# Moving the hgrn readout, the convolution and the low parts of some weights in a one-core encoder layer

## Chip, cores and metric

The kernel runs on one core of a Trainium2 chip. The metric is the device time of one execution in microseconds (us); the time before is the median of three runs.

## What is computed

One layer of a streaming encoder on 256 tokens of width 2048, all in float32. Cut to what matters here:

```
xn = rms_norm(x, g_mix)
cb, cc, ch, hq, hf, hi, hg, aq, ak, av, gate_a, gate_b, gate_c = split(xn @ w_in)
y_conv = cb * causal_depthwise_conv(cc * ch, conv_w)          # width 1024
y_hg   = hgrn2(hq, hf, hi, hg, ...)                           # width 1024
y_att  = chunk_band_attention(aq, ak, av, rel_bias)           # width 1024
merged = (sigmoid(gate_a) * (y_conv @ w_branch[0])
        + sigmoid(gate_b) * (y_hg   @ w_branch[1])
        + sigmoid(gate_c) * (y_att  @ w_branch[2]))           # width 2048
h = x + merged @ w_o
h = h + square(relu(rms_norm(h, g_ff) @ w_ff1)) @ w_ff2
h = h + sigmoid(rms_norm(h, g_ple) @ w_ple_gate) * (p @ w_ple_in)
out = rms_norm(h, g_final)
```

## The kernel before

**Arithmetic.** A float32 product is made of three matmuls in a narrower format: each operand is split into a high part (a rounded copy, made on ACT) and a low part (the operand less its high part, one subtraction on DVE), and the product is high x high + high x low + low x high (`mm_b` and `mm3`, lines 269 to 294). Activations are split once and kept (XN holds 16 blocks of 128 rows, each 256 tokens of high and 256 of low parts). Weights are split as they come.

**The weight stream.** The host packs all weights in the order of use (`units`, line 44). A unit is 128 x 1024 numbers, two units are one load of 1024 KB, issued by SP into one of three `raw` buffers (lines 165, 179). `Stream.unit` (line 162) splits a unit: ACT writes `hi` (line 192), DVE writes `lo` (line 193, by the helper of line 132). There are five buffers of each. `prod_a` (line 239) makes a 128-row block of columns from two units, `prod_t` and `prod_h` make rows of tokens. Each engine works through its instructions in a fixed order, which the framework draws up when the kernel is built from the order of the program and its own estimates of the durations; neighbouring pieces of work are therefore interleaved.

**Half a gate.** `prod_h` (line 346) multiplies XN by one half (1024 columns) of a gate's weights, in eight pairs of 128-row blocks, into PSUM banks: four `c`, and four `y` for the pairs in SEVEN = (1, 2, 4, 6). The other pairs are plain: two units of 12 matmuls each. A pair in SEVEN goes by `seven` (line 309): the 2 x 2 product of blocks (two row blocks by two column blocks) in seven block products instead of eight, with 21 matmuls. For that DVE forms differences of the weights (`tw`, lines 322, 327, 328) and four sets of low parts, and uses sums of activation blocks XS (`forms`, line 336), made once. It takes four of the hi and lo buffers. At the end of a half eight DVE operations combine c and y into `o` (lines 366 to 372).

**Stages.** First, in two groups of four heads, the projections for hgrn and attention with both computations beside them as side work (`side`, `step`). The attention outputs end each group (lines 687 to 694), and p1 and the PSUM pools are released. Then the convolution: eight blocks (lines 705 to 719), each with three products by `prod_a`, each result multiplied by rstd (`scaled`, line 462), which stands for the normalization's scale that XN does not yet hold. Then side work `rescale` (line 722) multiplies XN by rstd, splits it again in place and makes XS. Then the merge (lines 747 to 773): for the branches hg, at, cv in this order and two halves each, the gate's half by `prod_h(XN)`, its sigmoid on ACT, the branch's readout (`prod_h(branch, 4)`, eight plain units) and the product into `m`. In the first half the readout comes ahead of the gate, and ACT copies it into `m` (line 754). The output projection, the feed-forward part and the rest follow, and the change doesn't touch them.

`wide` and `narrow` take 2 KB tiles of the pool `ev` in turn (eight buffers).

Of the kernel before, what the change touches and what calls it, by code (L numbers as in the profile page):

```python
# [33 lines left out]
HALF = D // 2  # L34
GATES = ((1, "hg"), (2, "at"), (0, "cv"))

SEVEN = (1, 2, 4, 6)


C_CB, C_CC, C_CH, C_HQ, C_HF, C_HI, C_HG, C_AQ, C_AK, C_AV = [1024 * i for i in range(10)]  # L40
# [3 lines left out]
def units():  # L44

    def tile_a(name, row, col, n):
        return [("a", name, row + 1024 * j, col) for j in range(n)]

    def pair_a(name, row, c0, c1):
        return [("a", name, row, c0), ("a", name, row, c1),
                ("a", name, row + 1024, c0), ("a", name, row + 1024, c1)]

    def tile_b(name, col, row=0, n=8):
        return [("b", name, row + 256 * j, col) for j in range(n)]  # L60

    def half_b(name, col, row=0, n=8, seven=()):

        for g in range(n):
            r = row + 256 * g
            if g in seven:
                yield "c", name, (r, col), (r, col + 512)
                yield "c", name, (r + P, col + 512), (r + P, col)
            else:
                yield "b", name, r, col  # L70
                yield "b", name, r, col + 512

    out = []
    for g in range(2):
        out += tile_b("w_in", C_HI + 512 * g)
        for h in range(4 * g, 4 * g + 4):
            for c in (C_HQ, C_HF, C_HG):
                out += tile_a("w_in", 0, c + P * h, 2)
        for h in range(4 * g, 4 * g + 4):
            for c in (C_AQ, C_AK):  # L80
                out += tile_a("w_in", 0, c + P * h, 2)
        out += tile_b("w_in", C_AV + 512 * g)
    for i in range(8):
        for c in (C_CC, C_CH, C_CB):
            out += tile_a("w_in", 0, c + P * i, 2)
    for j, _ in GATES:
        for h in range(2):
            two = [half_b("w_in", (C_GA, C_GB, C_GC)[j] + HALF * h, seven=SEVEN),
                   half_b("w_branch", HALF * h, j * CW, 4)]
            for part in two[::-1] if j == GATES[0][0] and h == 0 else two:  # L90
                out += part
    for c in range(NC):
        out += tile_b("w_o", 512 * c)
    for f in range(NFG):
        out += pair_a("w_ff1", 0, f * 2048, f * 2048 + P)
        for i in range(2, FT):
            out += tile_a("w_ff1", 0, f * 2048 + P * i, 2)
        for c in range(NC):
            out += tile_b("w_ff2", 512 * c, f * 2048)
            if f == PLE_AT:  # L100
                out += tile_b("w_ple_in", 512 * c, 0, 1)
    for c in range(NC):
        out += tile_b("w_ple_gate", 512 * c)
    return out
# [3 lines left out]
def encoder_kernel(ctx: ExitStack, tc: tile.TileContext, xT, xtok, pT, wst, gains, gfin, convw, lblog,  # L108
# [4 lines left out]
    cst = ctx.enter_context(tc.tile_pool(name="cst", bufs=1))  # L113
    wp = ctx.enter_context(tc.tile_pool(name="wp", bufs=5))
    big = ctx.enter_context(tc.tile_pool(name="big", bufs=1))
    ev = ctx.enter_context(tc.tile_pool(name="ev", bufs=8))
    PS = bass.MemoryType.PSUM
    acc = tc.alloc_tile_pool(name="acc", bufs=4, space=PS, reuse_waits="tile")
    bgp = tc.alloc_tile_pool(name="bgp", bufs=2, space=PS, reuse_waits="tile")
# [29 lines left out]
    class Stream:  # L149
# [9 lines left out]
            self.n += 2  # L159
            return raw.rearrange("p a b -> p (a b)")  # L160

        def unit(self, hi=None, lo=None):
            r, half = divmod(self.n, 2)
            if half == 0:
                self.raw = wp.tile([P, 2, 1024], F32, name="raw", bufs=3)
                if r == 0:
                    for k in range(4):
                        a, b = divmod(k, 2)
                        w = slice(512 * b, 512 * b + 512)
                        nc.sync.dma_start(self.raw[:, a, w], wst[0, :, 512 * k:512 * k + 512])  # L170
                        if k == 0:
                            nc.sync.dma_start(gn, gains)
                        load_x(k, 1)
                elif r < 4:
                    for j in range(2):
                        load_x(4 * r + 2 * j, 2)
                        nc.sync.dma_start(self.raw[:, j, :], wst[r, :, 1024 * j:1024 * j + 1024])
                else:
                    nc.sync.dma_start(self.raw, wst[r].rearrange("p (a b) -> p a b", a=2))
            self.n += 1  # L180
            raw = self.raw[:, half, :]
            if hi is None:
                hi = wp.tile([P, 1024], F32R, name="hi")
            if lo is None:
                lo = wp.tile([P, 1024], F32R, name="lo")
            m = 2 if r < 4 else 1
            for j in range(m):
                w = slice(1024 // m * j, 1024 // m * (j + 1))
                if r < 4:
                    k = 4 * r + 2 * half + j  # L190
                    split(XN[:, k, :], xr[:, k, :], g_mix[:, k:k + 1])
                S.activation(hi[:, w], raw[:, w], AF.Copy)  # L192
                tt(lo[:, w], raw[:, w], hi[:, w].bitcast(F32), ALU.subtract)
            return hi, lo
# [148 lines left out]
        S.activation(xs[:, 0:4, :], f, AF.Copy)  # L343
        tt(xs[:, 4:8, :], f, xs[:, 0:4, :].bitcast(F32), ALU.subtract)

    def prod_h(x, n=8, xs=None):


        c = [acc.tile([P, 512], F32, name="ps") for _ in range(4)]
        y = None  # L350
        for g in range(n):
            if xs is not None and g in SEVEN:
                if y is None:
                    y = [acc.tile([P, 512], F32, name="ps") for _ in range(4)]
                seven(c, y, x, 2 * g, xs[SEVEN.index(g)], g == SEVEN[0], g == SEVEN[-1])
                step()
            else:
                for h in range(2):
                    unit = nxt()
                    for t in range(2):  # L360
                        mm_b(c[2 * t + h], unit, x, 2 * g, t, first=g == 0, last=g == n - 1)
                    step()
        if xs is None:
            return c
        o = [wide("o") for _ in range(4)]
        S.activation(o[0], y[0], AF.Copy)
        tt(o[1], y[2], o[0], ALU.add)
        tt(o[2], y[3], o[1], ALU.add)
        tt(o[1], y[1], o[1], ALU.add)
        tt(o[3], y[1], o[2], ALU.add)  # L370
        for i in range(4):
            tt(o[i], c[i], o[i], ALU.add)
        return o
# [327 lines left out]

    late = tc.alloc_tile_pool(name="late", bufs=1, reuse_waits="tile")
    p2 = tc.alloc_tile_pool(name="p2", bufs=1, reuse_waits="tile")
    ycv = late.tile([P, 8, 512], F32R, name="ycv", tag="c16")
    for i in range(8):
        u = p2.tile([P, 2 * T], F32, name="u")
        y = narrow("z")
        cc = wide()[:, 0:T]
        G.memset(u[:, 0:2], 0.0)
        scaled(cc)  # L710
        scaled(u[:, 2:T + 2])
        tt(u[:, 2:T + 2], u[:, 2:T + 2], cc, ALU.mult)
        V.tensor_scalar(y, u[:, 2:T + 2], cw[:, 2, i:i + 1], None, op0=ALU.mult)
        V.scalar_tensor_tensor(y, u[:, 1:T + 1], cw[:, 1, i:i + 1], y, op0=ALU.mult, op1=ALU.add)
        V.scalar_tensor_tensor(y, u[:, 0:T], cw[:, 0, i:i + 1], y, op0=ALU.mult, op1=ALU.add)
        cb = wide()[:, 0:T]
        scaled(cb)
        tt(y, y, cb, ALU.mult)
        split(ycv[:, i, :], y)
    XS = [p2.tile([P, 8, P], F32R, name=f"XS{i}") for i in range(len(SEVEN))]  # L720

    def rescale():

        for g in range(NK // 2):
# [8 lines left out]
                forms(XS[SEVEN.index(g)], a)  # L733
            yield

    side.append(rescale())

    M = [None] * 2

# [3 lines left out]
        S.activation(hi, pt, AF.Copy)  # L743
        tt(m[:, k:k + 2, T:2 * T], pt, hi.bitcast(F32), ALU.subtract)

    m = p2.tile([P, 2, D], F32, name="m")
    for i, (_, y) in enumerate(GATES):
        for h in range(2):
            first = i == h == 0
            branch = {"hg": yhg, "at": yat, "cv": ycv}[y]  # L750
            if first:

                for q, b in enumerate(prod_h(branch, 4)):
                    S.activation(m[:, q // 2, 512 * (q % 2):512 * (q % 2) + 512], b, AF.Copy)
            sg = prod_h(XN, xs=XS)
            for s in sg:
                S.activation(s, s, AF.Sigmoid)
            ps = None if first else prod_h(branch, 4)
            for t in range(2):
                for n in range(2):  # L760
                    c = HALF * h + 512 * n
                    dst, s = m[:, t, c:c + 512], sg[2 * t + n]
                    if first:
                        tt(dst, dst, s, ALU.mult)
                    elif i == 0:
                        tt(dst, ps[2 * t + n], s, ALU.mult)
                    else:
                        tt(s, ps[2 * t + n], s, ALU.mult)
                        tt(dst, dst, s, ALU.add)
            if i == 2:  # L770
                M[h] = big.tile([P, 8, 512], F32R, name=f"M{h}", tag="b16", bufs=2)
                for c in (2 * h, 2 * h + 1):
                    side.append(turn([m[:, t, 512 * c:512 * c + 512] for t in range(2)], c, put_m))
# [198 lines left out]
```

## Time and profile before

| | us |
|---|---|
| median of three runs | 1805.08 (1804.89 to 1809.15) |
| the profiled execution | 1807.12 |
| its span, first to last instruction | 1805.4 |
| PE busy in the span | 1784.2 |
| DVE busy | 1217.1 |
| ACT busy | 908.9 |
| POOL busy | 8.7 |

PE is the matmul engine (PEld its weight loads), DVE the vector engine, ACT the scalar engine, POOL the one that only sets constants here, SP the one that issues the loads. A matmul's row shows its modelled duration (0.39 us for 512 columns) although the next one starts before it ends: rates are read from the starts, and a PE that is called busy may still be waiting a little. "L226" is line 226 of the kernel. Names like `lo<-raw,hi` say what is written from what. The granted clock of PE is at its full level (0.998 of 2.4 GHz on the mean).

### The profile page before, as it was taken

To read this page: it belongs to the slowest core of one execution; us is meant where nothing else is said; L and a number is where in the kernel's file an instruction comes from. 1 tells how busy PE (TensorE), PEld (TensorE's weight loads), DVE (VectorE), ACT (ScalarE), POOL (GpSimd) and SP (SyncE) were. 2 spreads that over 40 slices of the span, in tenths; PEclk is the share of its full clock that TensorE was granted. 3 is DMA by queue.
4 is the path that set the end of the run, shared out by engine and by line. 5 is a ranking of instruction groups with operands and counts; after the bars stand their busy time and mean duration, and the time that the engine had idled before them with its cause. 6 is when DMAs were issued, how large, how long until landed. Compare 5 with 4: busy or idle time off the path is not lost.

```text
span 1805.4 us, 22667 instructions
## 1 busy us (share of the span) xinstructions
PE 1784.2 (99%) x8902; PEld 1505.0 (83%) x8902; DVE 1217.1 (67%) x1629; ACT 908.9 (50%) x1252; POOL 8.7 (0%) x56
## 2 busy tenths in 40 slices
PE   9999999999999999999999999999999999999997
PEld 7888888888876788888888888888888888888886
DVE  7686468666799888888755665566556655665564
ACT  7556455644455555564545443444444433444564
POOL 1000000000000000000000000000000000000000
PEclk9999999999999999999999999999999999999999
DMA  8544554345535655555665555555555555555452
GB/s 295 190 157 147 185 187 162 139 170 186 187 143 186 225 184 197 213 203 202 232 228 186 183 191 187 190 188 186 203 190 187 187 188 197 185 186 194 175 200 98
DMA packets 51083, 339.41 MB, mean 188 GB/s; under 512 B 6176, under 2 KB 7712, under 8 KB 10912
## 3 DMA queue, kind: packets, MB, share of 16 engines
q1 hardware_dynamic: 50976, 337.97, 52.0%
q8 instruction: 69, 1.13, 0.2%
q14 instruction: 38, 0.31, 0.1%
HBM read 335.85 MB, written 2.10 MB: 187 GB/s over the span
## 4 chain that ended last, share of the span: by engine, by line
PE 94%; DVE 4%; ACT 1%; issue 1%; DMA 0%; SPq 0%; ACTq 0%; DVEq 0%
PE ps L226 27%; PE ps L278 15%; PE ps L277 15%; PE ps L276 15%; PE ps L228 13%; PE ps L293 2%; PE ps L294 2%; PE ps L292 2%; DVE lo L132 1%; PE pl L507 1%; PE bg L396 1%; DVE tw L132 1%; DVE a L132 1%; ACT hi L192 0%; DMA raw<-wst 0%
## 5 line engine op out<-in xcount | busy, mean ns | idle before, releaser
L132 DVE TENSOR_TENSOR lo<-raw,hi 128x1024 fp32r<-128x1024 f32 (+1 forms) x630 | 744.1, 1189 | 522.5 <-ACT hi L192 518.0
L192 ACT ACTIVATE hi<-raw 128x1024 fp32r<-128x1024 f32 (+1 forms) x582 | 606.1, 1047 | 728.8 <-PE ps L278 335.4
L226 PE MATMUL ps<-XN,hi 128*128 128x512 f32 x1024 | 364.9, 401 | 0.0
L226 PE MATMUL ps<-XF,hi 128*128 128x512 f32 x1024 | 360.5, 397 | 0.0
L228 PE MATMUL ps<-XN,lo 128*128 128x256 f32 x1024 | 287.8, 281 | 0.0
L228 PE MATMUL ps<-XF,lo 128*128 128x256 f32 x1024 | 287.1, 281 | 0.0
L226 PEld LDWEIGHTS ps<-XN,hi 128*128 128x128 f32 x1024 | 192.4, 188 | 46.7
L226 PEld LDWEIGHTS ps<-XF,hi 128*128 128x128 f32 x1024 | 192.2, 188 | 46.6 <-DVE XF L208 0.2
L276 PE MATMUL ps<-hi,A 128*128 128x512 f32 x512 | 199.5, 390 | 0.0
L277 PE MATMUL ps<-lo,A 128*128 128x512 f32 x512 | 199.3, 389 | 0.0
L278 PE MATMUL ps<-hi,A 128*128 128x512 f32 x512 | 199.2, 389 | 0.0
L228 PEld LDWEIGHTS ps<-XF,lo 128*128 128x128 f32 x1024 | 193.5, 189 | 0.2
L228 PEld LDWEIGHTS ps<-XN,lo 128*128 128x128 f32 x1024 | 193.4, 189 | 0.2
L276 PE MATMUL ps<-hi,XN 128*128 128x512 f32 x320 | 125.7, 397 | 2.3 <-ACT XN L207 1.4
L277 PE MATMUL ps<-lo,XN 128*128 128x512 f32 x320 | 125.2, 391 | 1.8 <-DVE lo L132 1.8
L278 PE MATMUL ps<-hi,XN 128*128 128x512 f32 x320 | 125.0, 391 | 0.0
L276 PEld LDWEIGHTS ps<-hi,A 128*128 128x128 f32 x512 | 96.1, 188 | 19.9
L278 PEld LDWEIGHTS ps<-hi,A 128*128 128x128 f32 x512 | 96.1, 188 | 19.9
L277 PEld LDWEIGHTS ps<-lo,A 128*128 128x128 f32 x512 | 96.1, 188 | 19.8
L305 ACT ACTIVATE hi<-tw 128x1024 fp32r<-128x1024 f32 x48 | 50.9, 1060 | 65.7 <-DVE tw L132 34.9
L276 PEld LDWEIGHTS ps<-hi,XN 128*128 128x128 f32 x320 | 60.0, 188 | 16.7 <-ACT hi L192 2.6
L277 PEld LDWEIGHTS ps<-lo,XN 128*128 128x128 f32 x320 | 60.1, 188 | 15.3 <-DVE lo L132 3.0
(241 smaller groups left out, 2129.5 us busy)
## 6 DMA issues: line engine op xcount, KB each, us to landing
raw<-wst SPq DMA_DIRECT2D x310, 1024.0 KB, 4.8
raw<-wst SPq DMA_DIRECT2D x6, 512.0 KB, 7.5
hh<-xtok SPq DMA_DIRECT2D x2, 1024.0 KB, 6.4
out<-hh SPq DMA_DIRECT2D x8, 256.0 KB, 2.5
xr<-xT SPq DMA_DIRECT2D x6, 256.0 KB, 6.7
raw<-wst SPq DMA_DIRECT2D x4, 256.0 KB, 4.5
bias<-relb SPq DMA_DIRECT2D x8, 128.0 KB, 2.1
gf<-gfin SPq DMA_DIRECT2D x1, 1024.0 KB, 7.5
```

The source lines that it names most:

```text
L132: V.tensor_tensor(out_, a, b, op=op)
L192: S.activation(hi[:, w], raw[:, w], AF.Copy)
L226: PE.matmul(ps, hi[:, w], x[:, k, :], start=first and j == 0, stop=False, skip_group_check=True)
L228: PE.matmul(ps[:, 0:T], lo[:, w], x[:, k, 0:T], start=False, stop=last and j == nk - 1, skip_group_check=True)
L276: PE.matmul(ps, xh, hi[:, w], start=first and j == 0, stop=False)
L277: PE.matmul(ps, xh, lo[:, w], start=False, stop=False)
L278: PE.matmul(ps, xl, hi[:, w], start=False, stop=last and j == 1)
L292: PE.matmul(ps, x[0], w[0], start=first, stop=False)
L293: PE.matmul(ps, x[0], w[1], start=False, stop=False)
L294: PE.matmul(ps, x[1], w[0], start=False, stop=last)
L305: S.activation(hi[:, 0:n], w, AF.Copy)
L396: PE.transpose(pt[:, b, P * t:P * t + P], src[t][:, P * (2 * q + b):P * (2 * q + b) + P], ident)
```

## The change

- SEVEN becomes (1, 2, 3, 5, 6): five pairs of each gate half by seven multiplications instead of four.
- Both halves of the hgrn readout (`prod_h(yhg, 4)`) move to the place right behind the attention outputs, ahead of any gate; `rescale` runs as side work in them and is finished there.
- The convolution blocks move behind the gate halves of hgrn, four behind each. They read the rescaled XN, so the products by rstd go.
- With `adds`, the first unit of each plain pair (`h == 0`) gets its low part in another way: ACT writes the negated high part into `lo`, a transfer issued on POOL's queue adds `raw` to it, and ACT writes `hi`. This holds for the plain pairs of the gates and for all readouts.
- `ev` has seven buffers instead of eight; `u` comes from it. The weights are packed in the new order.

```diff
-SEVEN = (1, 2, 4, 6)
+SEVEN = (1, 2, 3, 5, 6)
...
-    for i in range(8):
-        for c in (C_CC, C_CH, C_CB):
-            out += tile_a("w_in", 0, c + P * i, 2)
+    for h in range(2):
+        out += half_b("w_branch", HALF * h, GATES[0][0] * CW, 4)
     for j, _ in GATES:
         for h in range(2):
-            two = [half_b("w_in", (C_GA, C_GB, C_GC)[j] + HALF * h, seven=SEVEN),
-                   half_b("w_branch", HALF * h, j * CW, 4)]
-            for part in two[::-1] if j == GATES[0][0] and h == 0 else two:
-                out += part
+            out += half_b("w_in", (C_GA, C_GB, C_GC)[j] + HALF * h, seven=SEVEN)
+            if j == GATES[0][0]:
+                for i in range(4 * h, 4 * h + 4):
+                    for c in (C_CC, C_CH, C_CB):
+                        out += tile_a("w_in", 0, c + P * i, 2)
+            else:
+                out += half_b("w_branch", HALF * h, j * CW, 4)
...
-    ev = ctx.enter_context(tc.tile_pool(name="ev", bufs=8))
+    ev = ctx.enter_context(tc.tile_pool(name="ev", bufs=7))
...
+            if adds:
+                assert r >= 4
+                S.activation(lo, raw, AF.Copy, scale=-1.0)
+                G.dma_start(lo, raw, accum_op=ALU.add)
+                S.activation(hi, raw, AF.Copy)
+                return hi, lo
...
-                    unit = nxt()
+                    unit = nxt(adds=adds and h == 0)
...
+    m = p2.tile([P, 2, D], F32, name="m")
+
     side.append(rescale())
+    for h in range(2):
+        for q, b in enumerate(prod_h(yhg, 4, adds=True)):
+            c = HALF * h + 512 * (q % 2)
+            S.activation(m[:, q // 2, c:c + 512], b, AF.Copy)
+    while side:
+        step()
+
+    ycv = late.tile([P, 8, 512], F32R, name="ycv", tag="c16")
+
+    def conv(i):
+        u = wide("u")
+        y = narrow("z")
+        G.memset(u[:, 0:2], 0.0)
+        cc = prod_a(XN)
+        step()
+        tt(u[:, 2:T + 2], prod_a(XN), cc, ALU.mult)
+        step()
...
+        tt(y, prod_a(XN), y, ALU.mult)
+        step()
+        split(ycv[:, i, :], y)
...
-            sg = prod_h(XN, xs=XS)
+            sg = prod_h(XN, xs=XS, adds=True)
             for s in sg:
                 S.activation(s, s, AF.Sigmoid)
-            ps = None if first else prod_h(branch, 4)
+            ps = prod_h({"at": yat, "cv": ycv}[y], 4, adds=True) if i else None
...
+            if i == 0:
+                for c in range(4 * h, 4 * h + 4):
+                    conv(c)
```

## Rows read from the trace of the kernel before

**Rows 1.** The page, busy us (share of the span) and instructions of each engine.

```profile
PE 1784.2 (99%) x8902; PEld 1505.0 (83%) x8902; DVE 1217.1 (67%) x1629; ACT 908.9 (50%) x1252; POOL 8.7 (0%) x56
```

**Rows 2.** Busy us (instructions) of each engine in stretches: convolution, readout, gate halves.

```profile
core 0: us, PE busy (x) PEld busy (x) DVE busy (x) ACT busy (x) POOL busy (x), PEclk, DMA share, GB/s
380.00:504.00 124.00, 124.00 (x703) 107.48 (x702) 88.03 (x132) 54.75 (x73) 0.70 (x7) 1.00 0.52 187
504.50:526.26 21.76, 21.76 (x99) 18.01 (x97) 21.07 (x40) 14.24 (x20) 0.00 (x0) 1.00 0.44 150
526.26:592.30 66.04, 60.47 (x248) 45.11 (x247) 64.68 (x82) 37.22 (x46) 0.00 (x0) 1.00 0.48 170
592.30:639.90 47.60, 47.60 (x211) 39.41 (x210) 40.14 (x45) 25.12 (x29) 0.00 (x0) 1.00 0.62 227
639.90:702.40 62.50, 62.50 (x277) 51.75 (x276) 53.81 (x59) 34.40 (x37) 0.00 (x0) 1.00 0.56 202
```

**Rows 3.** Timeline of PE: start, us, instruction; first readout to the third gate half.

```profile
504.49 0.40 PE L276 MATMUL ps<-hi,yhg 128*128 128x512 f32 x1
...
639.47 0.39 PE L278 MATMUL ps<-hi,yhg 128*128 128x512 f32 x1
639.70 0.39 PE L276 MATMUL ps<-hi,XN 128*128 128x512 f32 x1
...
645.14 0.39 PE L292 MATMUL ps<-hi,XN 128*128 128x512 f32 x1
```

**Rows 4.** Waits from 526 to 592: who waited for whom, total us, times, longest.

```profile
ACT hi L305 <- DVE tw L132: 18.5, 6, 4.7
PEld ps L293 <- DVE lo L132: 4.2, 8, 1.1
PEld ps L292 <- ACT hi L305: 4.0, 5, 1.0
```

**Rows 5.** Timeline of DVE from 558 to 686: start, us, instruction, idle before.

```profile
558.16 0.69 DVE L132 TENSOR_TENSOR XN<-a,XN 128x512 fp32r<-128x512 f32 x1
...
569.30 4.27 DVE L132 TENSOR_TENSOR o<-ps,o 128x512 f32<-128x512 f32 x7
...
668.92 1.22 DVE L132 TENSOR_TENSOR lo<-tw,hi 128x1024 fp32r<-128x1024 f32 x1 [0.96 <-ACT hi L305]
...
681.30 4.62 DVE L132 TENSOR_TENSOR lo<-raw,hi 128x1024 fp32r<-128x1024 f32 x4
```

**Rows 6.** Groups of instructions by form, 500 to 900: busy us, mean ns | idle before.

```profile
L192 ACT ACTIVATE hi<-raw 128x1024 fp32r<-128x1024 f32 x101 | 104.5, 1057 | 72.1 <-PE ps L278 62.8 <-PE ps L226 5.0 <-PE ps L294 1.7
```

**Rows 7.** The page's DMA issues: count, KB each, median us from issue to landing.

```profile
raw<-wst SPq DMA_DIRECT2D x310, 1024.0 KB, 4.8
raw<-wst SPq DMA_DIRECT2D x6, 512.0 KB, 7.5
...
out<-hh SPq DMA_DIRECT2D x8, 256.0 KB, 2.5
```

**Rows 8.** Waits from 592 to 805.

```profile
DVE lo L132 <- ACT hi L192: 14.0, 12, 1.5
...
DVE tw L132 <- DMA raw<-wst: 4.8, 6, 1.7
```

**Rows 9.** Timeline at the second group's attention outputs, DVE and PE.

```profile
365.77 1.22 DVE L132 TENSOR_TENSOR lo<-raw,hi 128x1024 fp32r<-128x1024 f32 x1 [2.07 <-ACT hi L192]
...
367.39 0.70 PE L690 MATMUL bg<-aw,av 128*128 128x256 f32 x2 [1.83 <-DVE yat L132]
```

**Rows 10.** Timeline of POOL in the convolution (one of six alike, 16.96 us apart).

```profile
420.36 0.10 POOL L709 MEMSET u<- 128x2 f32 x1 [16.86 <-DVE z L715]
```

**Rows 11.** Timeline of PE in the second gate half.

```profile
575.12 0.61 PE L292 MATMUL ps<-hi,XN 128*128 128x512 f32 x2
577.16 0.50 PE L277 MATMUL ps<-lo,XN 128*128 128x512 f32 x1 [1.42 <-DVE lo L132]
```

More of the change, by code (lines that the diff above doesn't have):

```diff
@@ L160, in whole, with unit @@
             return raw.rearrange("p a b -> p (a b)")
-        def unit(self, hi=None, lo=None):
+        def unit(self, hi=None, lo=None, adds=False):
             r, half = divmod(self.n, 2)
@@ L344, in forms, with prod_h @@
         tt(xs[:, 4:8, :], f, xs[:, 0:4, :].bitcast(F32), ALU.subtract)
-    def prod_h(x, n=8, xs=None):
+    def prod_h(x, n=8, xs=None, adds=False):
         c = [acc.tile([P, 512], F32, name="ps") for _ in range(4)]
@@ L703, in encoder_kernel @@
     p2 = tc.alloc_tile_pool(name="p2", bufs=1, reuse_waits="tile")
[L704 to L719, printed above, removed]
     XS = [p2.tile([P, 8, P], F32R, name=f"XS{i}") for i in range(len(SEVEN))]
@@ L734, in rescale @@
             yield
+    m = p2.tile([P, 2, D], F32, name="m")
     side.append(rescale())
+    for h in range(2):
[13 more added lines that the diff above has]
+        step()
+        V.tensor_scalar(y, u[:, 2:T + 2], cw[:, 2, i:i + 1], None, op0=ALU.mult)
+        V.scalar_tensor_tensor(y, u[:, 1:T + 1], cw[:, 1, i:i + 1], y, op0=ALU.mult, op1=ALU.add)
+        V.scalar_tensor_tensor(y, u[:, 0:T], cw[:, 0, i:i + 1], y, op0=ALU.mult, op1=ALU.add)
+        tt(y, prod_a(XN), y, ALU.mult)
+        step()
+        split(ycv[:, i, :], y)
     M = [None] * 2
@@ L744, in put_m @@
         tt(m[:, k:k + 2, T:2 * T], pt, hi.bitcast(F32), ALU.subtract)
-    m = p2.tile([P, 2, D], F32, name="m")
     for i, (_, y) in enumerate(GATES):
         for h in range(2):
[L749 to L754, printed above, removed]
-            sg = prod_h(XN, xs=XS)
+            sg = prod_h(XN, xs=XS, adds=True)
             for s in sg:
                 S.activation(s, s, AF.Sigmoid)
-            ps = None if first else prod_h(branch, 4)
+            ps = prod_h({"at": yat, "cv": ycv}[y], 4, adds=True) if i else None
             for t in range(2):
@@ L762, in encoder_kernel @@
                     dst, s = m[:, t, c:c + 512], sg[2 * t + n]
-                    if first:
+                    if i == 0:
                         tt(dst, dst, s, ALU.mult)
-                    elif i == 0:
-                        tt(dst, ps[2 * t + n], s, ALU.mult)
                     else:
@@ L769, in encoder_kernel @@
                         tt(dst, dst, s, ALU.add)
+            if i == 0:
+                for c in range(4 * h, 4 * h + 4):
+                    conv(c)
             if i == 2:
```

## The prediction

> **What bounds the kernel now.** I read the busy times first. PE is busy 99% of the span, DVE 67%, ACT 50% [rows 1]. So time is won in two ways only: fewer matmuls, or less time in which a busy-looking PE waits. For the second I read the table of stretches [rows 2]. From 592.30 on PE has no idle time in any stretch shown. From 526.26 to 592.30 it has 60.47 us of 66.04, and DVE has 64.68: there DVE is the limit.
>
> How much that costs is read from the first and last matmuls of the stretch [rows 3]. A 512-column matmul starts every 0.2267 us (24 of them between 639.70 and 645.14). A plain pair of 256 rows takes 24 (5.44 us), a pair by seven multiplications 21 (4.76 us). The first hgrn readout, both gate halves and the second readout are 96 + 180 + 180 + 96 = 552 matmuls, 125.1 us; they run from 504.49 to 639.70, 135.2 us. So **10.1 us are lost**. The next half, 276 matmuls, needs 62.6 us, and 639.70 to 702.40 is 62.7: nothing is lost there. The list of waits of the bad stretch names what PE waits for: DVE's low parts, and high parts on ACT [rows 4], which in turn wait for DVE's differences. DVE is late because the rescaling of XN and the sums XS still lie between its low parts long after the readout; one such row, a new XN, stands at 558.16 [rows 5].
>
> **The change, part by part.** In a run of work one 512-column operation of DVE costs 0.61 us and one 1024-column subtraction 1.15 (7 in 4.27, 4 in 4.62) [rows 5]. A seven pair is then 3 x 0.61 + 4 x 1.15 = 6.4 us of DVE, a plain pair 2 x 1.15 = 2.3, the eight combining operations of a half 4.9, the eight products and sums into m 4.9. As a test on the stretch from 639.90: 4 x 6.4 + 4 x 2.3 + 4.9 + 8 x 1.15 + 4.9 = 53.8; the row has 53.81 [rows 2].
>
> (a) *A fifth seven pair in each of six halves.* 18 matmuls fewer, 18 x 0.2267 = **-4.1 us**, all on PE.
>
> (b) *The rescaling moves under the readout.* Both halves of the hgrn readout now run together before any gate: 192 matmuls, 43.5 us of PE. DVE owes in it the rescaling (8 x 3 operations of 0.61 = 14.6), five sets of sums and splits (25 operations of at most 0.61: 15.3) and 8 low parts (9.2): at most 39.1. It fits, and every XN and XS is ready before a gate begins. The cause of the 10.1 us goes: **-10.1 us**. The bound from the other side is 0, if DVE's backlog only comes back later (rival 2). The gate halves for hgrn then need on DVE 5 x 6.4 + 3 x 1.15 + 4.9 + 2.4 = 42.8 against 40.1 of PE (105 + 72 matmuls). But four convolution blocks follow each; DVE is busy 88.03 of 124.00 us in the convolution now [rows 2], so the 67.8 us of four blocks (16.9 each, by the memsets that mark them [rows 10]) leave it 19 us, more than the 2.7 that spill over. Dropping 24 multiplications by rstd makes that larger; they lie off the path, and I cost them at nothing. The convolution's PE work is only moved, and so are its loads on SP's queue: in the weight stream they change places with the readout's. The memset of u stays on POOL, where transfers now queue behind it. It waits for an ev buffer of the block before, one block (16.9 us) ahead of its use, which is earlier than the transfers of the next gate are wanted. One buffer less in ev costs nothing as far as I see: eight are taken per convolution block, and the one that is taken again first (u) is dead by then.
>
> (c) *The adding transfers.* 42 of 512 KB (3 in each gate half, 4 in each of six readouts). Each takes 1.15 us from DVE and gives ACT one activation more, 1.06 us [rows 6]; ACT is busy 34.40 of 62.50 us, so 7 x 1.06 more per half is covered. In the plain units of a half DVE's account falls to 5 x 6.4 + 3 x 1.15 + 4.9 + 4 x 1.15 + 4.9 = 49.9 in 61.9 of PE. On the path lies the latency: the chain of such a lo is activation, issue on POOL, transfer, where it was activation and 1.15 us of DVE. No row has a POOL transfer or an adding one. The nearest: a store of 256 KB lands in 2.5 us, a load of 1024 KB in 4.8, loads of 512 KB in the crowded start in 7.5 [rows 7]. I take 4.8: the add reads two streams of 512 KB. Five lo buffers set what may be late. In a readout four units of 2.72 us lie between release and use, 10.9 us: hidden up to 9.8. After a seven pair its four tiles take 4.76 us, and the first use of lo is 0.23 later: 4.99. 1.06 + 4.8 is 0.9 too much. That place occurs twice in a half (pairs 4 and 7), 12 times: 10.4 us, if PE takes the units in program order; nothing, if it takes the other unit of the pair (2.72 us) first. **+5 us**, the middle, with 0 and 12 x (1.06 + 7.5 - 4.99) = 43 as ends.
>
> The Trainium skill prices such a transfer lower (DMA: Bandwidth & Descriptors, Anatomy of one DMA): about 2.0 us fixed on the GpSimd path plus the bytes at 436 GB/s, which is 3.2 us for 512 KB by that page, an estimate, and would leave no stall at all, a sum of -14.2. It is a fit of plain transfers, and no row here shows one from POOL.
>
> (d) *DVE's margin inside a gate half.* Its last low part of the last seven pair is done at 670.1 [rows 5]; PE wants it at 639.70 + 3 x 5.44 + 3 x 4.76 + 3.6 = 673.9, so 3.8 us in hand. In the new half DVE has 1.8 us more to do up to there (one more seven pair, four low parts fewer), PE is there 0.7 earlier: 1.3 us are left. No loss, **0**, but thin. Loads already arrive late for DVE now and then (4.8 us in 6 waits), and ACT holds it up for more [rows 8]; the transfers also share the DMA engines, 0.56 busy there. What it would cost is rival 2.
>
> (e) *At the attention outputs* PE waits 1.83 us while DVE does a unit's low part before yat's [rows 9]. An add in its place could free up to 1.8 us; the order may also keep it. I take 0.
>
> Sum: -4.1 - 10.1 + 5 = **-9.2 us**. Against the profiled execution, 1807.1 us (span 1805.4 and 1.7 around it), that is 1797.9; the median of the runs is 2.0 lower, so **1796**.
>
> **Rivals.** 1. *The transfers are quick enough.* If one lands in under 3.9 us, as the row of 2.5 us allows, (c) is 0: -14.2, 1791. This is the outcome of the skill's figure above. Against it: each byte is read twice, beside a weight stream.
>
> 2. *DVE becomes the bound of the gate halves.* The 1.3 us of (d) are eaten by late loads and by ACT's longer list. Two more DVE bubbles of 1.5 us in each half (the longest of its waits for ACT [rows 8]) overrun it by 1.7: 6 x 1.7 = 10 us come back, net -4 if the transfers are hidden: 1801, no measurable change. For it: the halves take five seven pairs in which DVE is slower than PE (6.4 against 4.76). Against: 12 us of DVE per half are free on the whole.
>
> 3. *Slower: the adds are late.* Place: pairs 4 and 7 of each half, PE at its first matmul on lo. Price: 12 x (latency + 1.06 - 4.99). At 5.1 us it has used up the 14.2 won; from 5.6 on the kernel is slower by over 0.3%; at 7.5, the upper row, 43 us are lost and the result is 1834. It needs program order on PE as well. Against it: where DVE is late PE's order already takes a later unit first (a seven pair's high part at 575.12, ahead of a plain unit's low part that it waits for until 577.16 [rows 11]). The Trainium skill (SBUF — State Buffer, Who interferes with whom) adds a reason for lateness, that transfers of the GpSimd queue can be held up while VectorE has the port they share, but takes its two-operand operation, almost all that DVE does here, out of that rule by inference; no row here shows either.
>
> 4. *The change doesn't do what it says:* the rescaling, emitted as side work, is placed behind the low parts as now, and the first gate still waits. Then -4.1 + 5: 1806. Against it: nothing but the readout is there to run in those 43.5 us.
>
> **Numbers.** A measurement of this kernel can tell about 0.3% (5.4 us) from no change. Chances: forecast 0.48, rival 1 0.12, rival 2 0.18, rival 3 0.16, rival 4 0.06. So faster 0.60, same 0.24, slower 0.16. The range runs from 1788 (rival 1 with the 1.8 us of (e), and a little) to 1811, which holds rivals 2 and 4 and the mild end of 3; most of rival 3 stays outside. The cases that are faster have 1788 to 1799.
>
> **What would show it.** Right: 18 matmuls fewer; PE without idle time in the first gate half and no XN operation on DVE after the readout (b); 42 transfers on a POOL queue, landing in 4 to 5.5 us (c); PE's waits on DMA of lo under 1 us each. Rival 2 would show as PE waiting for DVE lo or ACT hi in several halves; rival 3 as PE waiting for transfers into lo before pairs 4 and 7. The forecast is wrong if PE's lost time between the attention outputs and the output projection is over 15 us, or if the transfers slow the weight loads so that PE waits for raw.

## The result, and the profile after

The changed kernel takes **1855.8 us** (median; 1854.7 to 1856.5) where the kernel before takes 1805.2 on the same chip: ratio 1.0274, 95% interval 1.0258 to 1.0291. It is slower by 50.6 us; forecast were 1796 us, with a range from 1788 to 1811. The profiled execution took 1855.9 us, its span is 1854.1.

The page of the changed kernel: busy us of each engine, then DMA issues with their us to landing.

```profile
PE 1802.6 (97%) x8884; PEld 1504.2 (81%) x8884; DVE 1186.9 (64%) x1598; ACT 956.2 (52%) x1311; POOL 45.0 (2%) x98
...
raw<-wst SPq DMA_DIRECT2D x310, 1024.0 KB, 4.8
lo<-raw POOLq DMA_DIRECT2D x42, 512.0 KB, 5.9
```

Against [rows 1], PE has the 18 matmuls fewer that were promised, DVE 30 us less and ACT 47 us more; POOL, which only set constants, now issues 42 transfers. A transfer lands after 5.9 us (median), the weight loads after 4.8 as before [rows 7]. So by work done the change is what it says. The loss is idle time of PE. Take the stretch behind the attention outputs, up to the first matmul of the output projection. Its first row and the row behind its end, PE of the kernel before, then of the changed one:

```profile
368.72 0.48 PE L226 MATMUL ps<-XN,hi 128*128 128x512 f32 x1
...
893.01 0.48 PE L276 MATMUL ps<-hi,M 128*128 128x512 f32 x1
```

```profile
368.84 0.48 PE L288 MATMUL ps<-hi,yhg 128*128 128x512 f32 x1
...
940.21 0.48 PE L288 MATMUL ps<-hi,M 128*128 128x512 f32 x1
```

Before, it lasted 524.3 us, of which 10.1 were lost as read from [rows 3]. So its matmuls need 514.2 us, and with 18 fewer 510.2. After, it lasts 571.4 us: **61 us are lost in it instead of 10**.

Stretches of the changed kernel: the hgrn readout, a gate half of hgrn, four convolution blocks, a gate half of at, its readout, the next gate half, the last readout (columns as in [rows 2]).

```profile
368.84:412.90 44.06, 43.96 (x195) 36.06 (x194) 17.05 (x21) 28.10 (x36) 5.10 (x6) 1.00 0.88 246
412.90:458.18 45.28, 42.63 (x179) 32.83 (x178) 37.48 (x41) 28.25 (x31) 1.83 (x3) 1.00 0.60 204
458.18:525.79 67.61, 67.61 (x385) 58.61 (x384) 48.19 (x68) 32.27 (x43) 1.17 (x4) 1.00 0.61 211
641.59:686.76 45.17, 42.89 (x181) 32.96 (x180) 37.48 (x43) 30.00 (x35) 3.44 (x4) 1.00 0.61 188
686.76:712.27 25.51, 23.22 (x95) 18.69 (x94) 9.11 (x11) 12.40 (x15) 2.58 (x3) 0.93 0.95 274
712.27:763.59 51.32, 45.99 (x180) 33.68 (x179) 42.11 (x49) 29.18 (x33) 3.44 (x4) 0.97 0.57 182
911.01:940.20 29.19, 24.89 (x107) 20.02 (x106) 13.39 (x17) 13.91 (x17) 2.58 (x3) 0.94 0.83 251
```

The hgrn readout, with the rescaling under it, and the convolution lose next to nothing. Every gate half (177 matmuls, 40.1 us) takes 45 to 51, and every readout of at and cv (96 matmuls, 21.8 us) 25 to 29; of the 61 us some 42 lie in the six halves and 19 in the four readouts. Two columns stand out in a readout: the granted clock is 0.93 or 0.94, and the DMA engines are busy 0.95 and 0.83 of the time, where the readout of [rows 2] had a clock of 1.00 and a DMA share of 0.44.

Waits of the changed kernel from 362 to 940: who waited for whom, total us, times, longest.

```profile
PEld ps L289 <- DMA lo<-raw: 34.5, 18, 4.6
PE ps L289 <- DMA lo<-raw: 26.8, 17, 4.2
DVE tw L134 <- DMA raw<-wst: 23.2, 4, 6.9
ACT lo L194 <- DMA raw<-wst: 16.7, 7, 3.3
PEld ps L305 <- DVE lo L134: 10.8, 19, 1.1
```

PE waits for the adding transfers: 27 us in 17 waits (one wait shows as the matmul's and again as its weight load's; the two are not added). That is less than half of the 61. DVE waits four times, up to 6.9 us, for weights; in the same stretch of the kernel before, seven such waits made 5.7 us, the longest 1.7.

How one such wait comes about at pair 4 of the first gate half: ACT, POOL and PE in the timeline of the changed kernel.

```profile
429.54 1.06 ACT L317 ACTIVATE hi<-tw 128x1024 fp32r<-128x1024 f32 x1 [3.08 <-DVE tw L134]
430.50 1.04 ACT L196 ACTIVATE hi<-raw 128x1024 fp32r<-128x1024 f32 x1
431.45 1.04 ACT L194 ACTIVATE lo<-raw 128x1024 fp32r<-128x1024 f32 x1
...
432.79 0.87 POOL L195 DMA_DIRECT2D lo<-raw  x1 [29.04 <-ACT lo L194]
...
432.94 1.28 PE L288 MATMUL ps<-hi,XN 128*128 128x512 f32 x4
...
434.75 0.50 PE L289 MATMUL ps<-lo,XN 128*128 128x512 f32 x1 [0.24 <-DVE lo L134]
...
437.39 0.50 PE L289 MATMUL ps<-lo,XN 128*128 128x512 f32 x1 [0.99 <-DMA lo<-raw]
```

ACT's list is in order. The negation (L194) stands behind the unit's high part and behind a high part of the seven pair before it, for which ACT has waited 3.08 us on DVE. It starts at 431.45, though PE wants the pair from 432.94 on. From there it takes 1.0 us, POOL's issue follows 0.3 later, and the transfer lands at about 437.3, 4.5 us on. PE goes out of the program's order, taking four high-part matmuls and the other unit first, and still waits.

And how a late readout goes on, in the chain of waits of the changed kernel from 676 to 736 (start, us, what).

```profile
683.00 7.33 DMA raw<-wst
...
691.79 6.00 DMA lo<-raw
...
697.85 9.62 DMA raw<-wst
...
707.50 1.24 DVE tw L134
```

The transfer reads `raw`, so it holds one of three buffers until it has landed. SP issues the next load (697.85) only then; that load takes 9.62 us instead of 4.8, and DVE starts the next gate half's differences behind it at 707.50. That gate half is the one of 51.3 us.

### The profile page after: what moved, and what is told of

Its sections match the earlier page's. It is cut to its first block, busy times and chain, and to the rows that moved or that the text cites. A ratio compares the mean times of both kernels' runs of the same rounds, so it can differ in the third digit from the quotient of the medians.

```text
span 1854.1 us, 22885 instructions
## 1 busy us (share of the span) xinstructions
PE 1802.6 (97%) x8884; PEld 1504.2 (81%) x8884; DVE 1186.9 (64%) x1598; ACT 956.2 (52%) x1311; POOL 45.0 (2%) x98
## 4 chain that ended last, share of the span: by engine, by line
PE 84%; DMA 7%; DVE 4%; issue 3%; ACT 2%; SPq 0%; ACTq 0%; POOL 0%; POOLq 0%; DVEq 0%
PE ps L238 26%; PE ps L240 13%; PE ps L289 13%; PE ps L290 13%; PE ps L288 13%; DMA lo<-raw 4%; DMA raw<-wst 3%; DVE lo L134 2%; PE ps L305 1%; PE ps L306 1%; PE ps L304 1%; PE pl L519 1%; DVE tw L134 1%; DVE o L134 1%; PE bg L408 0%
## 5 line engine op out<-in xcount | busy, mean ns | idle before, releaser
L134 DVE TENSOR_TENSOR lo<-raw,hi 128x1024 fp32r<-128x1024 f32 (+1 forms) x588 | 690.9, 1181 | 545.3 <-ACT hi L204 541.6
L204 ACT ACTIVATE hi<-raw 128x1024 fp32r<-128x1024 f32 (+1 forms) x528 | 550.1, 1045 | 657.9 <-PE ps L290 288.5
L240 PE MATMUL ps<-XN,lo 128*128 128x256 f32 x1024 | 287.8, 281 | 0.0
L240 PE MATMUL ps<-XF,lo 128*128 128x256 f32 x1024 | 286.4, 280 | 0.0
L240 PEld LDWEIGHTS ps<-XN,lo 128*128 128x128 f32 x1024 | 193.4, 189 | 0.3
L240 PEld LDWEIGHTS ps<-XF,lo 128*128 128x128 f32 x1024 | 193.1, 189 | 0.2
L289 PE MATMUL ps<-lo,XN 128*128 128x512 f32 x272 | 110.5, 406 | 16.5 <-DMA lo<-raw 13.6
L290 PE MATMUL ps<-hi,XN 128*128 128x512 f32 x272 | 106.0, 397 | 0.0
L288 PE MATMUL ps<-hi,XN 128*128 128x512 f32 x272 | 104.1, 403 | 1.8 <-ACT XN L219 1.6
L317 ACT ACTIVATE hi<-tw 128x1024 fp32r<-128x1024 f32 x60 | 63.5, 1059 | 77.8 <-issue 31.2
L134 DVE TENSOR_TENSOR lo<-tw,hi 128x1024 fp32r<-128x1024 f32 x60 | 72.9, 1220 | 29.0 <-ACT hi L317 28.4
L289 PEld LDWEIGHTS ps<-lo,XN 128*128 128x128 f32 x272 | 51.9, 191 | 36.3 <-DMA lo<-raw 18.6
```

The costliest lines, as they stand in the source:

```text
L134: V.tensor_tensor(out_, a, b, op=op)
L240: PE.matmul(ps[:, 0:T], lo[:, w], x[:, k, 0:T], start=False, stop=last and j == nk - 1, skip_group_check=True)
L288: PE.matmul(ps, xh, hi[:, w], start=first and j == 0, stop=False)
L289: PE.matmul(ps, xh, lo[:, w], start=False, stop=False)
L290: PE.matmul(ps, xl, hi[:, w], start=False, stop=last and j == 1)
L317: S.activation(hi[:, 0:n], w, AF.Copy)
```

## The experiments

All are edits of the changed kernel. "Lost" is the length of the stretch named above in the profiled execution, less the time of its matmuls (510.2 us with five seven pairs, 514.2 with four). It is read from one execution, whose time can differ from the median by some us (1840.0 and 1844.3 with adds in the readouts).

| kernel | median us | ratio to before [95%] | stretch us | lost us |
|---|---|---|---|---|
| changed kernel | 1855.8 | 1.0274 [1.0258, 1.0291] | 571.4 | 61 |
| no adds | 1803.4 | 0.9980 [0.9971, 0.9989] | 520.9 | 10.7 |
| no adds, four seven pairs | 1798.1 | 0.9951 [0.9937, 0.9966] | 514.2 | 0.0 |
| adds in the gates (18) | 1828.9 | 1.0119 [1.0102, 1.0136] | 544.7 | 34.5 |
| of these: pair 0 (6) | 1806.0 | 0.9991 [0.9982, 1.0000] | 520.8 | 10.6 |
| of these: pairs 4, 7 (12) | 1827.9 | 1.0113 [1.0098, 1.0129] | 544.8 | 34.6 |
| the same on the pair's second unit | 1812.7 | 1.0034 [1.0021, 1.0046] | 528.9 | 18.7 |
| adds in the readouts (24) | 1844.3 | 1.0205 [1.0189, 1.0222] | 555.5 | 45.3 |
| of these: pairs 1 to 3 (18) | 1833.6 | 1.0145 [1.0131, 1.0159] | 546.0 | 35.8 |
| the 24, raw not held | 1836.9 | 1.0174 [1.0159, 1.0190] | 549.9 | 39.7 |
| the 24 as plain copies | 1824.8 | 1.0101 [1.0084, 1.0118] | 538.7 | 28.5 |

**Without any adding transfer**, everything else kept:

```
-        for q, b in enumerate(prod_h(yhg, 4, adds=True)):
+        for q, b in enumerate(prod_h(yhg, 4)):
...
-            sg = prod_h(XN, xs=XS, adds=True)
+            sg = prod_h(XN, xs=XS)
...
-            ps = prod_h({"at": yat, "cv": ycv}[y], 4, adds=True) if i else None
+            ps = prod_h({"at": yat, "cv": ycv}[y], 4) if i else None
```

> The changed kernel with every low part made by a subtraction on DVE again; the new order and five seven pairs stay. Theory A (the adding transfers are the whole loss: PE waits for their lo, the raw buffers they hold make the weight loads late, and the clock falls after the long waits): the 10.1 and 4.1 us of the prediction show, less 1 to 2 us in each of six halves, since DVE's work up to the last seven pair grows by 4.1 us against 3.8 in hand: 1797 to 1803 us. Theory B (five seven pairs overload DVE, and the transfers only relieve it): slower than the changed kernel, over 1856.

1803.4 us. The transfers cost 52.4 us together (1855.8 - 1803.4); order and fifth pair without them are 0.2% faster than before.

**And with four seven pairs again**, so that only the new order is left:

```
-SEVEN = (1, 2, 3, 5, 6)
+SEVEN = (1, 2, 4, 6)
```

> As the run before, with four seven pairs (1, 2, 4, 6) as in the kernel before: the new order alone. A: the stall of the first gate halves is gone and nothing else has changed: 1805.2 - 10.1 = 1795 us, within 2. B says nothing of four pairs; a third theory, that the new order itself costs (the convolution between the gates, seven ev buffers), gives 1805 or more.

1798.1 us, 0.5% faster than before, where the kernel before took 1807.1 beside it: the new order is worth 9 us, the 10.1 lost in the stretch are gone, and **the fifth seven pair costs 5.3**. Waits of PE and PEld from 365 to 880 without adds, with five pairs:

```profile
PE ps L240 <- DVE lo L134: 3.4, 2, 1.7
...
PEld ps L305 <- DVE lo L134: 3.1, 7, 0.5
```

With four, PE has no wait there but the one of 1.1 us at the attention outputs. A gate half of each (columns as above; first five pairs, then four):

```profile
635.20:676.04 40.84, 40.79 (x179) 32.98 (x178) 38.13 (x44) 26.42 (x30) 0.00 (x0) 1.00 0.51 180
```

```profile
629.26:670.07 40.81, 40.81 (x182) 33.80 (x181) 36.23 (x41) 25.78 (x29) 0.00 (x0) 1.00 0.56 201
```

The half with 177 matmuls takes as long as the one with 180: the 0.7 us are lost in small waits, most of them for DVE's low parts inside the seven pairs (L305). After the two hgrn halves PE also waits 1.7 us for the convolution's first low part (L240), which DVE can only make behind its combining operations and its products into m (from 450.69 to 457.5 after the first half).

**The adds in the gates alone** (readouts without):

> Adding transfers in the plain pairs of the gates alone (18 instead of 42), five seven pairs. A: PE's waits for lo in the gates stay (13.6 us in the trace of the changed kernel), the loads are no longer late behind the readouts: 1805 - 14 + 14 + 0 to 6 for the clock and DVE = 1805 to 1812. B: within 5 us of the changed kernel or slower, as DVE gets 24 low parts of 1.15 us back.

1828.9 us, 25.5 more than without adds; 1812 was the most that was expected. **In the readouts alone** (gates without):

> Adding transfers in the readouts alone (24), five seven pairs. A: PE's waits for lo in the readouts stay (13.2 us in the trace of the changed kernel), with the late loads and most of the low clock behind them: 1805 - 14 + 13 + 15 to 25 = 1819 to 1830. B: DVE's account of a gate with 6 more low parts overruns: over 1856.

1844.3 us, 40.9 more. Each was put too low, and the two together (66) are more than the 52.4 of the whole. A reason may be that a late transfer costs less where PE is late anyway; no run shows it.

**The gates' adds divided by place**: pair 0 alone, pairs 4 and 7 alone.

```
-                    unit = nxt(adds=adds and h == 0)
+                    unit = nxt(adds=adds and h == 0 and xs is not None and g == 0)
```

> Five seven pairs, an adding transfer for the first unit of pair 0 of each gate half only (6 in all). Theory A1 (what a transfer costs depends on how many matmuls of PE lie between the release of its lo buffer and the first use; in front of pair 0 there are four units of 2.72 us, 10.9, and the transfers of the run with adds in the gates land in 4.7): hidden, and DVE has 1.15 us less to do before the last seven pair, so the 0.7 us that each half lost without adds shrinks: 1798 to 1803. Rival A2 (every transfer costs about 25.5 / 18 = 1.4 us wherever it stands, through the DMA engines or POOL): 1803.4 + 8.5 = 1812.

```
+                    unit = nxt(adds=adds and h == 0 and xs is not None and g > 0)
```

> Five seven pairs, adding transfers for the first units of pairs 4 and 7 of each gate half only (12 in all), the places behind a seven pair. A1: nearly the whole loss of the run with adds in the gates (25.5 us over the run without) stands here: 1824 to 1830. A2: two thirds of it, 1820.

1806.0 us with the six of pair 0, which land after 6.2 us without any wait of PE for them; 1827.9 with the twelve of pairs 4 and 7, which land after 4.5. So in the gates it is not the transfer that costs but its place. Pairs 4 and 7, behind a seven pair, carry the whole loss of the gates, 24.5 / 12 = 2.0 us each. One hope failed: with pair 0's subtraction taken off DVE, the first three halves still take 40.8 us, as without adds. Then the same twelve on **the second unit of the pair**:

```
+                    unit = nxt(adds=adds and h == 1 and xs is not None and g > 0)
```

> The 12 adding transfers of the gate halves' pairs 4 and 7 alone, but on the second unit of the pair instead of the first. Both units come in one load, and PE reaches the second unit 12 matmuls (2.7 us) later, while ScalarE starts its negation about 1 us later. Theory L (PE waits because the landing is late, some 2.1 us at each of 12 places, and whatever follows from that wait): the slack of some 1.7 us takes most of the wait away, 1805 to 1815 us where the first unit gave 1827.9. Theory C (each transfer costs PE or VectorE about 2 us wherever it stands in these pairs): 1824 to 1830 us.

1812.7 us: 15.2 of the 24.5 are back, from a use that lies 12 matmuls (2.7 us) later. Waits of PE's weight loads from 365 to 890, adds on the first unit and on the second:

```profile
PEld ps L289 <- DMA lo<-raw: 19.7, 12, 2.8
PEld ps L289 <- DVE lo L134: 6.5, 12, 0.7
PEld ps L305 <- DVE lo L134: 4.9, 11, 0.6
PEld ps L288 <- ACT hi L204: 3.9, 9, 0.6
```

```profile
PEld ps L289 <- DMA lo<-raw: 15.1, 11, 2.3
PEld ps L305 <- DVE lo L134: 3.1, 6, 0.6
```

The waits for the transfers fall by only 4.6 us. The rest is what went with them: with the first unit late, PE takes the second unit, and a block of the next stage, before DVE and ACT have them; in the second kernel those rows are gone. In sum these rows are 35.0 against 18.2 us; the difference is near that of the stretches, 15.9.

**The readouts' adds divided**: pairs 1 to 3 alone, so that none is wanted at the start of a readout.

```
+                    unit = nxt(adds=adds and h == 0 and xs is None and g > 0)
```

> Five seven pairs, adding transfers in the readouts for the first units of pairs 1, 2 and 3 only (18 instead of 24). A1: the first pair of a readout stands behind a gate, where the loads, the lo buffers and three transfers fall together, and PE waits 3.3 to 4.4 us there; without it 10.9 us are free before each use against 8.4 of landing and 1.06 of ACT: 1803 to 1812. A2: three quarters of the 41 us of the run with adds in the readouts: 1834.

1833.6 us, 30.2 more than without adds: three quarters of the transfers cost three quarters of the 40.9. Here it is not the place alone. They land after 7.6 us, PE waits for four of them at the first use (2.4 to 3.0 us), and DVE then waits for weights. Two things of the transfer are left: it holds `raw`, and it shares the DMA engines. **The first is taken away** by another source:

```
-                G.dma_start(lo, raw, accum_op=ALU.add)
+                G.dma_start(lo, adds.bitcast(F32), accum_op=ALU.add)
...
-                    unit = nxt(adds=adds and h == 0)
+                    unit = nxt(adds=x[:, 0:2, :].rearrange("p a b -> p (a b)") if adds and h == 0 else None)
```

> The 24 adding transfers of the readouts alone, with the same destinations, sizes and places, but their source is the readout's own activation block and no longer the raw buffer (so the low parts of these units are not those of the weights). The raw buffer is now free as soon as ScalarE and VectorE have read it. Theory H: what cost 41 us with raw as the source (1844.3 us against 1803.4 without adds) is mostly that the transfer holds one of three raw buffers until it lands, so that the next load starts late and VectorE, the next gate half and PE follow. Then SP no longer waits for the landing of lo, raw loads start in time, what is left are the first waits of the four readouts of at and cv (3.3 to 4.4 us each), and the time is 1808 to 1824 us. Theory T: the queues themselves are too full for the extra 512 KB, whoever holds what: landing and loads stay late, 1834 to 1848 us.

1836.9 us, 7.4 less (5.6 by the stretches). SP no longer waits for a transfer into lo (before, 23 waits), and the gate halves behind a readout are back at what they are without adds, 40.9 us for the second gate half of at where that kernel has 41.1. That half with `raw` held, then with the other source (columns as above):

```profile
702.61:745.97 43.36, 42.19 (x179) 32.68 (x177) 41.92 (x49) 26.44 (x30) 0.85 (x1) 1.00 0.49 169
```

```profile
704.66:745.54 40.88, 40.74 (x178) 32.97 (x177) 39.43 (x45) 26.81 (x30) 0.85 (x1) 1.00 0.51 175
```

But the readouts of at and cv still lose 7 to 9 us each (6 to 9 before). So holding `raw` is the smaller part. **The adding itself** is taken away next, same source, queue and size:

```
-                G.dma_start(lo, raw, accum_op=ALU.add)
+                G.dma_start(lo, raw.bitcast(F32R))
```

> The 24 transfers of the readouts alone, as in the kernel that took 1844.3 us, with the same source, destination, size and queue, but as plain copies: nothing is added, so the destination is written and not read as well (the low parts of these units are then the raw weights). Theory D (the adding is what makes them long, 2.6 us of all 16 DMA engines each, where half a weight load takes about 1.4): the copies land in 4 to 6 us in the same traffic, PE's first waits in the readouts of at and cv fall under 1.5 us, and the time is 1806 to 1820 us. Theory T (any 512 KB on POOL's queue beside the weight loads lands that late): 7.5 to 9 us to landing, 1834 to 1848 us.

1824.8 us, between the two: 19.5 of the 40.9 us go, and a readout of at and cv loses 3 to 5 us instead of 6 to 9. The 21.4 that plain copies still cost (`raw` held, the same bytes beside the loads, one more activation on ACT) are not divided further. The transfers from 362 to 940 (POOL's queue: packets, MB, share of 16 engines; then issues and median us to landing), first adding, then copying:

```profile
q0 software_dynamic: 3279, 11.92, 10.8%
...
lo<-raw POOLq DMA_DIRECT2D x22, 512.0 KB, 8.5
```

```profile
q0 software_dynamic: 3312, 12.06, 5.8%
...
lo<-raw POOLq DMA_DIRECT2D x22, 512.0 KB, 6.5
```

For the same bytes the adding takes nearly twice the time of the DMA engines: 10.8% of 578 us over 22.7 transfers (11.92 MB at 0.524 each) is 2.7 us of all 16, against 1.5. What that does to the weights is seen in ten microseconds of the first at readout, with the adding transfers and without any (columns as above; the last is GB/s):

```profile
680.00:690.00 10.00, 9.91 (x37) 7.74 (x36) 1.22 (x1) 3.07 (x3) 1.88 (x3) 0.83 0.96 227
```

```profile
680.00:690.00 10.00, 10.00 (x46) 8.29 (x45) 7.27 (x7) 3.46 (x5) 0.00 (x0) 1.00 0.93 355
```

The engines are as busy, and move 227 GB/s instead of 355. In a readout all units are plain and PE takes 1 MB of weights every 5.44 us; there the DMA engines have the least to spare. These are ten dense microseconds; the whole readout without transfers:

```profile
676.04:697.80 21.76, 21.76 (x97) 18.02 (x96) 18.27 (x21) 9.40 (x11) 0.00 (x0) 1.00 0.66 242
```

The engines are busy for 14.4 of its 21.8 us. Four adding transfers ask for 4 x 2.7 = 10.8 more, 25.2 in all, which is more than the readout lasts; four copies ask for 6.0, 20.4 in all. These sums are estimates from the shares. They bind where a transfer can't start ahead: the hgrn readouts of the changed kernel, whose first transfer is issued at 354.39, 14 us before them, lose next to nothing.

**POOL subtracts instead** of a transfer, in all 42 places:

```
-                S.activation(lo, raw, AF.Copy, scale=-1.0)
-                G.dma_start(lo, raw, accum_op=ALU.add)
                 S.activation(hi, raw, AF.Copy)
+                G.tensor_tensor(lo, raw, hi.bitcast(F32), op=ALU.subtract)
```

> The changed kernel with the 42 transfers replaced by a subtraction on POOL (hi on ACT, then raw less hi on POOL), at the same places. A1 (latency decides): POOL's subtraction has no row here; if it takes 2 to 3 us, the chain fits the 4.99 us behind a seven pair and the weight stream has the DMA engines to itself: 1795 to 1803. If DVE, which reads two operands as well, and POOL hold each other up, DVE's rows get longer than 1.22 us and the time is above the run without adds: 1804 to 1830.

1818.3 us (ratio 1.0060 [1.0042, 1.0079]). One subtraction takes 2.7 us, so it is never as late as a transfer; PE waits 4.9 us in all for POOL. But DVE stands still beside it. Its timeline at the attention outputs, with POOL's, ACT's and PE's (this kernel's line numbers are one lower behind the edit):

```profile
360.29 2.82 POOL L195 TENSOR_TENSOR lo<-raw,hi 128x1024 fp32r<-128x1024 f32 x1 [2.45 <-ACT hi L194]
...
360.77 2.88 DVE L134 TENSOR_TENSOR XN<-a,XN 128x512 fp32r<-128x512 f32 x1
...
364.49 0.63 ACT L724 ACTIVATE XN<-a 128x512 fp32r<-128x512 f32 x1 [4.29 <-DVE a L134]
...
365.70 0.68 DVE L134 TENSOR_TENSOR XN<-a,XN 128x512 fp32r<-128x512 f32 x1
...
368.02 2.08 PE L701 MATMUL bg<-aw,av 128*128 128x256 f32 x4 [3.48 <-ACT av L394]
```

The same operation takes 0.68 us alone (365.70) and 2.88 beside POOL's subtraction (360.77), and two other rows there show the same; ACT's list waits for it, PE for ACT, and the hgrn readout begins at 375.99 instead of 368.84; part of that is PE's granted clock, which is 1.2 GHz from 366.90 to 377.14. This makes 7 of the 14.9 us over the kernel without adds; the stretch itself takes 526.8 us, 6.0 more than there. The Trainium skill states this (SBUF — State Buffer, Who interferes with whom): a DVE instruction with two SBUF inputs contends with a GpSimd instruction that reads SBUF. The trace agrees.

**A better kernel than the new order alone?** Four pairs in the hgrn halves, five in the others, and there one subtraction (pair 0) on POOL:

```
-SEVEN = (1, 2, 3, 5, 6)
+SEVEN = (1, 2, 4, 5, 6)
+FOUR = (1, 2, 4, 6)
...
-            sg = prod_h(XN, xs=XS, adds=True)
+            sg = prod_h(XN, xs=XS, sv=SEVEN if i else FOUR)
...
+                    unit = nxt(adds=xs is not None and sv is SEVEN and g == h == 0)
```

> The new order without any adding transfer; four seven pairs (1, 2, 4, 6) in the hgrn gate halves, five (1, 2, 4, 5, 6) in the four gate halves of at and cv, and there the first unit of pair 0 has its low part subtracted on POOL (2.73 us) instead of on VectorE (1.22 us). Theory P: VectorE was the bound of the five-pair halves by 0.7 us each; with 1.2 us taken off it, each of the four halves comes down to PE's 40.1 us, 0.7 us less than with four pairs, and the hgrn halves keep the four-pair kernel's zero loss: 1798.1 - 4 x 0.7 = 1795.3 us (1794.5 to 1796.5). Rival V: VectorE is slowed beside POOL, or late at another place, and the fifth pair again gives nothing: 1797.5 to 1800 us.

1798.7 us (ratio 0.9961 [0.9949, 0.9974]); the rival holds. The four halves with five pairs take 40.8 us or more again, with small waits for ACT's high parts and DVE's low parts spread over them. **The new order with four pairs and no transfers, 1798.1 us, has the lowest time found**, 0.5% below the kernel before; the intervals of the two overlap, so the one with five pairs can't be told from it.

## Why the prediction was wrong, by its own steps

- **(c) failed, in two places: how long a transfer has to land, and how long it takes beside the loads of a readout.** It said +5, with 43 as the upper end; measured are +52. *In the gates* the place (pairs 4 and 7, twelve times) was right and so was the landing (4.8 taken, 4.5 measured). Wrong was the time to hide it in. "4.99 us from release to use" took the freeing of the lo buffer as the start. In the trace the negation starts 1.5 us ahead of the pair's first matmul (431.45 and 432.94; with adds at pairs 4 and 7 alone, 1.5 to 1.8 in 11 of the 12 places), since ACT's list has the unit's high part and a wait for DVE ahead of it. And going out of program order was taken to save PE ("nothing, if it takes the other unit first"): PE did so and still lost 2.0 us a place, 25 in all. *In the readouts* "hidden up to 9.8" failed on both sides. In the kernel with adds in the readouts alone, the first negation of the at readout starts at 669.55 and PE wants the low part at 674.86, right behind the matmul of 674.63: 5.3 us later instead of 10.9. And a transfer lands after 8.5 us (median), not 4.8: loads and adds together ask for more of the DMA engines than a readout lasts (25.2 us in 21.8, an estimate from the shares above). The prediction named the engines as shared, 0.56 busy, for the gate halves in (d), put no cost on it and made no such sum for a readout. With adds in the readouts alone this cost 41 us, the larger part.

  ACT and PE of that kernel at the first such place:

```profile
669.55 1.04 ACT L194 ACTIVATE lo<-raw 128x1024 fp32r<-128x1024 f32 x1
...
674.63 0.39 PE L288 MATMUL ps<-hi,yat 128*128 128x512 f32 x1
...
678.97 0.50 PE L289 MATMUL ps<-lo,yat 128*128 128x512 f32 x1 [3.95 <-DMA lo<-raw]
```

- **Rival 3** had the right place and wait in the gates, with 0.16: late transfers, at pairs 4 and 7. But its 43 us needed a landing of 7.5 and program order on PE; the 25 us there came at 4.5 and out of that order. It had no word on the readouts. **Rival 1** fell: no adding transfer landed in under 4.4 us, where it needed 3.9. The mark "over 15 us lost means the forecast is wrong" was passed four times over, and the other, that the transfers slow the weight loads until work waits for raw, came true by way of other engines: DVE waits 23.2 us for raw and ACT's negations 16.7.
- **The Trainium skill's figure** in (c) (DMA: Bandwidth & Descriptors, Anatomy of one DMA), an estimate of 3.2 us for 512 KB, was too low as a median in every stretch: the traces have 4.5 at pairs 4 and 7 and 8.5 in the readouts for adding, 6.5 for plain copies. The quickest of the 24 plain copies landed after 3.1.
- **(b) was right**: -10.1 predicted, and the new order alone lost nothing in the stretch (10.1 before) and took 1798.1 us where the kernel before took 1807.1 beside it, 9.0 less. In the changed kernel DVE writes the last new XN at 373.08, where it was 558.16 [rows 5], so rival 4 falls. The rescaling doesn't run under the readout only, as was said: it begins at 345.06, ahead of it.
- **(a) and (d) belong together.** The 18 matmuls are gone, but the 4.1 us were gained in no run: without adds the five-pair halves are no shorter, and the fifth pair costs 5.3 us on top of the 4.1. (d)'s "1.3 us are left" counted on two subtractions a half that the transfers take off DVE; without them its account is 1.0 us short (3.8 - 4.1 - 0.7), and a half loses 0.7. That looks like rival 2, a bound by DVE. But with pair 0's subtraction off DVE the account is level (1.15 more) and the half still takes 40.8, so the sum of DVE's work doesn't explain these waits; their cause inside the halves stays open, and whether (d) would hold with transfers that are in time no run shows. Over half of the 9.4 us (4.1 and 5.3) lies at the convolution, whose two stretches take 3.5 and 1.9 us longer than with four pairs. For it (b) had counted 19 us of free DVE time on the mean and not what stands ahead of DVE's first low part there.
- **(e)** 0 holds: the hgrn readout starts at 368.84, 368.89 and 368.34 with and without adds, where the convolution started at 368.72.

## What to carry to other kernels

Before work is moved from a busy engine to a DMA, read the time between the moment the data is *really* ready (behind everything in that engine's list) and its use, and compare it with the landing in the stretch where it will run. A transfer out of a load buffer lengthens the buffer's life, so it delays loads as well. And where another engine is nearly full (DVE is busy 38 of the 41 us of a five-pair half), saving matmuls on PE at the price of more work there may give nothing: here the change of order was worth 0.5%, and each of the two parts put on top of it made the kernel slower.

## What the runs showed of the hardware

- An adding transfer from SBUF to SBUF of 512 KB takes 2.7 us of all 16 DMA engines, a plain copy 1.5. It lands after 4.5 us at pairs 4 and 7 of a gate half, after 8.5 in a readout (medians).
- PE's granted clock fell to 1.2 GHz behind waits. In the changed kernel, around the wait that ends at 694.43 (columns as above):

```profile
691.75:695.06 3.31, 1.02 (x4) 0.48 (x3) 1.23 (x1) 1.64 (x2) 0.87 (x1) 0.98 1.04 345
695.06:697.62 2.56, 2.56 (x7) 1.97 (x6) 0.00 (x0) 2.00 (x2) 0.85 (x1) 0.50 1.06 261
```

  In the second row matmuls start 0.43 us apart instead of 0.2267. There are five such spells in the stretch, some 40 matmuls in all, some 8 us of the 61; each begins within 2 us of the end of a wait of 2.2 to 4.2 us. One wait of 2.8 us was followed by none, and with adds at pairs 4 and 7 alone one spell, from 454.43, came behind a wait of only 0.9. The kernel before has no such spell in this stretch.
- POOL's `tensor_tensor` of 128 x 1024 takes 2.7 us on the mean. Most DVE operations of 512 or 1024 columns with both inputs in SBUF that begin beside it end 0.5 or 1.1 us after it, so they take up to 2.9 us. One with an input in PSUM isn't held: `o<-ps,o` at 681.47 takes 0.68 beside it.
